# Weight splits held behind a norm's vector steps, the mean square summed on ScalarE, attention weights scaled on ScalarE

## The chip, the core and the metric

The kernel runs on one core of a Trainium2 chip. The core has a matrix engine (TensorE; PE in the profile, PEld being its weight loads), a vector engine (VectorE, DVE), an engine for activations (ScalarE, ACT), a general one (GpSimd, POOL) and one that only issues transfers (SyncE, SP). Each engine works through its own queue in order, and they wait for one another by semaphores. The metric is the device time of one execution in microseconds.

## What is computed

Two transformer blocks, 256 tokens of width 1024, everything in fp32. The first block has two layers, the second one. Cut to what matters here:

```python
for l in range(2):                                   # first block
    h = rms_norm(x, g_pre_mix[l])
    q, k, v, cb, cc, cx, ga, gb = split(h @ w_in[l])
    y_attn = band_attention(rope(q), rope(k), v, sink[l]) @ w_attn_proj[l]
    y_conv = (cb * short_conv(cc * cx, conv_w[l])) @ w_conv_proj[l]
    mix = (sigmoid(ga) * y_attn + sigmoid(gb) * y_conv) @ w_out[l]
    x = x + rms_norm(mix, g_post_mix[l])
    h = rms_norm(x, g_pre_ffn[l])
    x = x + rms_norm((silu(h @ w_gate[l]) * (h @ w_up[l])) @ w_down[l], g_post_ffn[l])
# second block: the same frame, norms modulated by a condition vector
# (h = rmsnorm(x) * (1 + scale) + shift), stick-breaking attention and a pooling mixer

def rms_norm(x, g):
    return x * rsqrt(mean(x * x, axis=-1) + 1e-6) * g

# in band_attention, per block of 128 queries and head
p = exp(sc - m)
denom = sum(p, axis=-1) + exp(sink - m)
o = (p / denom) @ v
```

## The kernel before

**Weights.** All weights are packed into a list of chunks of 128 x 2048 fp32 (1 MB), in the order of their use (`ORDER`). `emit_raw` (L242) loads a chunk into one of four buffers on SyncE's queue. `emit_split` (L252) splits it into a high part H (rounded to the matrix engine's fp32r by ScalarE, L265) and a low part L (the rest, a subtraction on VectorE, L266), in two halves of 128 x 1024; there are nine buffers for halves of H and nine for L. A product is then three matmuls: high by high, low by high, high by low. `get(key)` (L271) hands out the next chunk, and before that emits the loads up to five chunks ahead (`LOOK_RAW`) and the splits up to three ahead (`LOOK`, counting the chunk itself). Chunks called `cond` belong to the second block's condition and are not split: VectorE sums them (L490), GpSimd reduces the sum (L493).

**Order.** The program is traced in one order, and a scheduler then places each engine's instructions: among those that its own timing model has ready it takes the one with the earliest place in the program, as far as buffers allow. `hp()` moves the norm steps 30 places forward. Work that comes from generators (transposes, attention units) is traced into TensorE's stream at due times of a clock that counts matmul time (`spawn`, `tick`); TensorE's order is that of the trace.

**A boundary.** There are five places at which an output product is followed by a norm, the residual, another norm and the next weights: mixer to FFN in layers 0 and 1 (`mix_out`, L461), FFN to the next mixer after layers 0 and 1 (`ffn`, L496), and the second block's output projection to its FFN (L951 to L965). `row_out` (L450) ends the output product for the first row tile of 128 tokens, then for the second one. After each half of the columns `Post.half` squares the result on ScalarE (`sumsq`, L331, tiles `jk_a..`) and multiplies it by the gain (L391, `ag`). After a row tile, `after` calls `post.fin` (inverse root on GpSimd: `rstd`, L333, three small operations `ms`, `m` and `rs`; then x is updated, L398) and `Norm.vec` (squares of x, L331; gain, L356, `xg`; inverse root; scale, L360 or L362), and spawns the transposes of that tile (`Norm.tr`, L371, `pt_n..`) for 6 us later by the program's clock (`TR_DELAY`). The transposed rows are split again (`Pair.put`, L201 and L202). The FFN starts with chunks `gA` and `uA` (two each), each used for both row tiles.

**Attention.** `attention` (L560) spawns eight units per layer, one per group of four heads and row tile, every 10 us of the clock. A unit splits and transposes q (`qs`, `qT`), computes scores S, masks them and takes the maximum on VectorE, takes four exponentials of 128 x 256 on ScalarE with their sums (L628), one more of the sink (L630, `es`), the reciprocal on VectorE (L631, L633, `rd`), multiplies the four tiles P by it on GpSimd (L635), transposes P on TensorE (L643, `PTp`) 8 us of the clock later, and multiplies by v. The units run between the matmuls of the convolution branch (`pcc`, `pcx`, `pcb`).

## Time and profile before

| | us |
|---|---|
| three timed runs, median (lowest, highest) | 1191.44 (1191.36, 1191.72) |
| the profiled execution, device time | 1194.28 |
| its span, first to last instruction | 1192.4 |
| TensorE busy | 1159.4 (97%) |
| VectorE busy | 773.1 (65%) |
| ScalarE busy | 618.3 (52%) |
| GpSimd busy | 129.1 (11%) |

The page gives busy times for the whole span. A busy TensorE says that a matmul was in work, not that it ran at full clock, so the granted clock is read beside it. A row of a timeline has the start, the time from the start of the first to the end of the last of its merged instructions, the engine, the line, the operation with its output and inputs, and in brackets how long the engine was idle before it and who ended that. Successive instructions overlap a little at their ends.

### The profile page before, as it was taken

To read this page: it belongs to the slowest core of one execution; us is meant where nothing else is said; L and a number is where in the kernel's file an instruction comes from. 1 tells how busy PE (TensorE), PEld (TensorE's weight loads), DVE (VectorE), ACT (ScalarE), POOL (GpSimd) and SP (SyncE) were. 2 spreads that over 40 slices of the span, in tenths; PEclk is the share of its full clock that TensorE was granted. 3 is DMA by queue.
4 is the path that set the end of the run, shared out by engine and by line. 5 is a ranking of instruction groups with operands and counts; after the bars stand their busy time and mean duration, and the time that the engine had idled before them with its cause. 6 is when DMAs were issued, how large, how long until landed. Compare 5 with 4: busy or idle time off the path is not lost.

```text
span 1192.4 us, 17771 instructions
## 1 busy us (share of the span) xinstructions
PE 1159.4 (97%) x7144; PEld 1029.3 (86%) x7144; DVE 773.1 (65%) x958; ACT 618.3 (52%) x927; POOL 129.1 (11%) x146
## 2 busy tenths in 40 slices
PE   6999999999999999999999999999999999999997
PEld 4899888878999987998888878999988777999996
DVE  6768655769576747677747768776858448655542
ACT  5756556555444346656556555344455546544441
POOL 1012300011202001022220022020211002000000
PEclk9999999999999999999999999999999999999999
DMA  8743344757676665634438547675866345655620
GB/s 307 284 135 114 111 147 177 271 181 259 231 258 239 226 233 181 243 106 142 142 142 316 185 169 257 230 290 180 315 230 222 120 159 177 247 177 177 206 77 36
DMA packets 36250, 235.50 MB, mean 197 GB/s; under 512 B 4668, under 2 KB 5180, under 8 KB 9416
## 3 DMA queue, kind: packets, MB, share of 16 engines
q1 hardware_dynamic: 33696, 225.41, 53.2%
q10 hardware_dynamic: 2472, 8.96, 2.3%
q8 instruction: 56, 0.92, 0.3%
q14 instruction: 26, 0.21, 0.1%
HBM read 233.28 MB, written 1.07 MB: 197 GB/s over the span
## 4 chain that ended last, share of the span: by engine, by line
PE 51%; POOL 2%; ACT 1%; DVE 1%; issue 1%; POOLq 0%; ACTq 0%; DVEq 0%
PE pu L236 10%; PE dn L236 9%; PE pg L236 8%; PE wo L236 2%; PE pcp L236 2%; PE pap L236 2%; PE pga L236 2%; PE pgb L236 2%; PE pcx L236 2%; PE pcb L236 1%; PE puA L236 1%; PE pgA L236 1%; PE z L236 1%; PE po L236 1%; PE pv L236 1%
## 5 line engine op out<-in xcount | busy, mean ns | idle before, releaser
L266 DVE TENSOR_TENSOR L<-raw,H 128x1024 fp32r<-128x1024 f32 x374 | 470.1, 1264 | 218.6 <-ACT H L265 207.7
L265 ACT CAST H<-raw 128x1024 fp32r<-128x1024 f32 x374 | 391.0, 1050 | 321.3 <-PE pu L236 71.5
L236 PE MATMUL dn<-H,fHL 128*128 128x512 f32 x432 | 116.4, 391 | 0.0
L236 PEld LDWEIGHTS dn<-H,fHL 128*128 128x128 f32 x432 | 79.8, 188 | 15.6
L635 POOL TENSOR_SCALAR P<-P,rd 128x256 f32<-128x256 f32 x64 | 48.2, 769 | 228.9 <-DVE rd L633 83.7
L236 PE MATMUL dn<-L,fHL 128*128 128x512 f32 x216 | 66.8, 390 | 0.0
L493 POOL PARTITION_ALL_REDUCE mrow<-cacc x6 | 40.1, 6675 | 219.5 <-DVE cacc L490 180.8
L490 DVE SCALAR_TENSOR_TENSOR cacc<-raw,silu_c,cacc 128x1024 f32<-128x1024 f32 x48 | 61.4, 1280 | 0.3
L236 PEld LDWEIGHTS dn<-L,fHL 128*128 128x128 f32 x216 | 40.5, 188 | 8.5
L536 DVE TENSOR_TENSOR f<-pu,s 128x512 f32<-128x512 f32 x27 | 18.6, 690 | 30.1 <-PE pu L236 30.1
L628 ACT ACTIVATE P<-S,nm 128x256 f32<-128x256 f32 x64 | 29.6, 478 | 11.8 <-DVE nm L622 11.8
L539 ACT CAST fHL<-f 128x512 fp32r<-128x512 f32 x27 | 16.8, 622 | 36.1 <-DVE f L536 36.1
L236 PE MATMUL pg<-xf2H,H 128*128 128x256 f32 x144 | 35.4, 283 | 0.0
L236 PE MATMUL pg<-xf0H,H 128*128 128x256 f32 x144 | 35.4, 283 | 0.0
L236 PE MATMUL pg<-xf1H,H 128*128 128x256 f32 x144 | 35.3, 283 | 0.0
L236 PE MATMUL pu<-xf0H,H 128*128 128x256 f32 x144 | 35.3, 283 | 0.0
L236 PE MATMUL pu<-xf0L,H 128*128 128x256 f32 x144 | 35.3, 283 | 0.0
L236 PE MATMUL pu<-xf1H,H 128*128 128x256 f32 x144 | 35.3, 283 | 0.0
L236 PE MATMUL pu<-xf1L,H 128*128 128x256 f32 x144 | 35.3, 283 | 0.0
L236 PE MATMUL pu<-xf2H,H 128*128 128x256 f32 x144 | 35.3, 283 | 0.0
L236 PE MATMUL pu<-xf2L,H 128*128 128x256 f32 x144 | 35.3, 283 | 0.0
L236 PE MATMUL pg<-xf0L,H 128*128 128x256 f32 x144 | 35.3, 283 | 0.0
(402 smaller groups left out, 2928.2 us busy)
## 6 DMA issues: line engine op xcount, KB each, us to landing
raw<-in_wpack_dram SPq DMA_DIRECT2D x209, 1024.0 KB, 5.0
raw<-in_wpack_dram SPq DMA_DIRECT2D x4, 512.0 KB, 8.9
gpm<-in_gains_dram ACTq DMA_DIRECT2D x3, 512.0 KB, 6.0
gpf<-in_gains_dram ACTq DMA_DIRECT2D x3, 512.0 KB, 7.0
gqf<-in_gains_dram ACTq DMA_DIRECT2D x2, 512.0 KB
out_dram<-x SPq DMA_DIRECT2D x4, 256.0 KB, 2.1
pmat<-in_pmat_dram SPq DMA_DIRECT2D x2, 384.0 KB, 5.6
x<-in_x_dram SPq DMA_DIRECT2D x2, 256.0 KB, 2.6
```

The costliest lines, as they stand in the source:

```text
L236: nc.tensor.matmul(o, a, b, start=start, stop=stop, **kw)
L265: nc.scalar.copy(H, rv)
L266: nc.vector.tensor_sub(L, rv, H.bitcast(F32))
L490: nc.vector.scalar_tensor_tensor(a3, w[:, k], silu_c[:, 2 * j + k:2 * j + k + 1], a3, ALU.mult, ALU.add)
L493: nc.gpsimd.partition_all_reduce(mrow, a, P, bass_isa.ReduceOp.add)
L536: nc.vector.tensor_mul(f, pu, s)
L539: nc.scalar.copy(fHL[:, 0], fv)
L628: nc.scalar.activation(Pt[:, hh, :], S[hh // 2][:, hh % 2, :], AF.Exp, bias=nm[:, hh:hh + 1], accum_out=den[:, hh:hh + 1])
L635: nc.gpsimd.tensor_scalar(Pt[:, hh, :], Pt[:, hh, :], rd[:, hh:hh + 1], 0.0, ALU.mult, ALU.add)
```

## The change

`get` takes a second argument that limits how far ahead it splits: at the five boundaries the output product's chunks are split, and nothing behind them. A new function `split_ahead` splits the next two chunks, and is called in `after` for the first row tile, once its `Norm.vec` has been traced; `issue_after` orders the casts on ScalarE behind the last instruction of that norm's sum of squares, and the subtractions on VectorE behind the last scaling. `sumsq` scales x by 1/32 inside the square, and a second ScalarE instruction on 128 x 1 (Identity with a bias) adds epsilon or the first half's sum; on GpSimd only the power is left. The multiplication of the attention weights goes from GpSimd to ScalarE.

```diff
@@ -268,16 +268,24 @@
             HL[i] = hv
         state["spl"] += 1
 
-    def get(key):
+    def get(key, look=LOOK):
         i = state["use"]
         assert ORDER[i] == key, (ORDER[i], key)
         n = len(ORDER)
         while state["raw"] < min(i + LOOK_RAW, n):
             emit_raw()
-        while state["spl"] < min(i + LOOK, n):
+        while state["spl"] < min(i + min(look, LOOK), n):
             emit_split()
         state["use"] += 1
         return HL.pop(i)
+
+    def split_ahead(*behind):
+
+        with ExitStack() as st:
+            for ins in behind:
+                st.enter_context(tc.issue_after(ins.ins))
+            while state["spl"] < min(state["use"] + LOOK - 1, len(ORDER)):
+                emit_split()
 
 
     HC = [slice(0, 512), slice(512, 1024)]
@@ -300,6 +308,8 @@
     nc.sync.dma_start(xt[1], x_in[P:2 * P, :])
     nhalf = cst.tile([P, 1], F32, tag="nhalf", name="nhalf")
     nc.vector.memset(nhalf, -0.5)
+    eps = cst.tile([P, 1], F32, tag="eps", name="eps")
+    nc.vector.memset(eps, EPS)
     ident_r = cst.tile([P, P], F32R, tag="identr", name="ident_r")
     nc.vector.tensor_copy(ident_r, ident)
     modd = dr.tile([6, D], F32, tag="modd", name="modd")
@@ -327,16 +337,15 @@
 
 
     def sumsq(src, c, ssq, name):
+
         junk = s2(f"jk_{name}{c}")
-        nc.scalar.activation(junk, src, AF.Square, accum_out=ssq[:, c:c + 1])
+        nc.scalar.activation(junk, src, AF.Square, scale=D ** -0.5, accum_out=ssq[:, c:c + 1])
+        return nc.scalar.activation(ssq[:, c:c + 1], ssq[:, c:c + 1], AF.Identity,
+                                    bias=eps if c == 0 else ssq[:, 0:1])
 
     def rstd(ssq, name):
-        ms = small("ms_" + name, 1)
-        nc.gpsimd.tensor_scalar(ms, ssq[:, 0:1], 1.0 / D, EPS, ALU.mult, ALU.add)
-        m2 = small("m2_" + name, 1)
-        nc.gpsimd.tensor_scalar(m2, ssq[:, 1:2], 1.0 / D, ms[:, 0:1], ALU.mult, ALU.add)
         rs = small("rs_" + name, 1)
-        nc.gpsimd.tensor_tensor(rs, m2, nhalf, ALU.pow)
+        nc.gpsimd.tensor_tensor(rs, ssq[:, 1:2], nhalf, ALU.pow)
         return rs
 
     class Norm:
@@ -352,14 +361,14 @@
                 ssq = small("sx_" + name, 2)
                 xg = s4("xg_" + name)
                 for c in range(2):
-                    sumsq(xt[t][:, HC[c]], c, ssq, "x" + name)
+                    self.sq = sumsq(xt[t][:, HC[c]], c, ssq, "x" + name)
                     nc.vector.tensor_mul(xg[:, HC[c]], xt[t][:, HC[c]], self.G[:, HC[c]])
                 rs = rstd(ssq, "x" + name)
                 for c in range(2):
                     if self.S is None:
-                        nc.vector.tensor_scalar(xg[:, HC[c]], xg[:, HC[c]], rs[:, 0:1], None, ALU.mult)
+                        self.sc = nc.vector.tensor_scalar(xg[:, HC[c]], xg[:, HC[c]], rs[:, 0:1], None, ALU.mult)
                     else:
-                        nc.vector.scalar_tensor_tensor(xg[:, HC[c]], xg[:, HC[c]], rs[:, 0:1], self.S[:, HC[c]],
+                        self.sc = nc.vector.scalar_tensor_tensor(xg[:, HC[c]], xg[:, HC[c]], rs[:, 0:1], self.S[:, HC[c]],
                                                        ALU.mult, ALU.add)
             self.h = xg
 
@@ -461,13 +470,14 @@
     def mix_out(l, kts, mp, make_post, after, lead):
         accs = [[ps1(f"wo{l}_{t}{c}") for c in range(2)] for t in range(2)]
         for i, j in enumerate(kts[:lead]):
-            w = get(("wo", l, j))
+            w = get(("wo", l, j), len(kts) - i)
             tick()
             for t in range(2):
                 for c in range(2):
                     mmD2(accs[t], w, mp.ks(0, 2 * j, 2), mp.ks(1, 2 * j, 2), t, c, i == 0, False)
         drain()
-        ch = [(get(("wo", l, j)), mp.ks(0, 2 * j, 2), mp.ks(1, 2 * j, 2)) for j in kts[lead:]]
+        ch = [(get(("wo", l, j), len(kts) - i), mp.ks(0, 2 * j, 2), mp.ks(1, 2 * j, 2))
+              for i, j in enumerate(kts) if i >= lead]
         row_out(ch, accs, lead > 0, make_post, after)
 
     cacc = [None]
@@ -550,7 +560,7 @@
                         for c in range(2):
                             mmD2(accs[t], w, fs[j][0], fs[j][1], t, c, j == 0, False)
                 else:
-                    tail.append((get(key), fs[j][0], fs[j][1]))
+                    tail.append((get(key, NDOWN - j), fs[j][0], fs[j][1]))
         if l == DEPTH - 1:
             with tc.issue_after(last.ins):
                 nc.scalar.preload_act_table_set("natural_log_exp_and_others")
@@ -632,7 +642,7 @@
             rd = small(f"rd{l}{g}{t}", 4)
             nc.vector.reciprocal(rd, den)
             for hh in range(4):
-                nc.gpsimd.tensor_scalar(Pt[:, hh, :], Pt[:, hh, :], rd[:, hh:hh + 1], 0.0, ALU.mult, ALU.add)
+                nc.scalar.activation(Pt[:, hh, :], Pt[:, hh, :], AF.Copy, scale=rd[:, hh:hh + 1])
             yield SM_DELAY
             if t == 0:
                 PT[g] = [s4(f"PT{l}{g}{pr}", (P, 2, 2, T)) for pr in range(2)]
@@ -879,6 +889,8 @@
         def after(t, post):
             post.fin()
             norms[t].vec()
+            if t == 0:
+                split_ahead(norms[t].sq, norms[t].sc)
             spawn(norms[t].gen, TR_DELAY)
 
         mix_out(l, [0, 1, 2, 3], mp, lambda t, acc: Post(t, acc, gpm, f"pm{l}{t}"), after, LEAD)
@@ -909,6 +921,8 @@
         def after2(t, post):
             post.fin()
             nn[t].vec()
+            if t == 0:
+                split_ahead(nn[t].sq, nn[t].sc)
             spawn(nn[t].gen, TR_DELAY)
 
         ffn(l, xp, norms, mkpost, after2)
@@ -946,6 +960,8 @@
     def after3(t, post):
         post.fin()
         norms[t].vec()
+        if t == 0:
+            split_ahead(norms[t].sq, norms[t].sc)
         spawn(norms[t].gen, TR_DELAY)
 
     accs = [[ps1(f"wo2_{t}{c}") for c in range(2)] for t in range(2)]
@@ -954,7 +970,7 @@
         for c in range(2):
             mmD2(accs[t], *pw[i], t, c, i == 0, False)
     drain()
-    aw = [(get(("wo", 2, j)), mp.ks(0, 2 * j, 2), mp.ks(1, 2 * j, 2)) for j in (0, 1)]
+    aw = [(get(("wo", 2, j), 2 - j), mp.ks(0, 2 * j, 2), mp.ks(1, 2 * j, 2)) for j in (0, 1)]
     for t in range(2):
         post = Post(t, accs[t], Pm, f"pm2{t}")
         left = pw[max(0, WO2_LEAD - 2):] if t == 1 else []
```

## Rows read from the trace of the kernel before

**Rows 1.** The page, part 1: busy us, share of the span, instructions.

```profile
PE 1159.4 (97%) x7144; PEld 1029.3 (86%) x7144; DVE 773.1 (65%) x958; ACT 618.3 (52%) x927; POOL 129.1 (11%) x146
```

**Rows 2.** TensorE's waits: who for whom, us in total, times, longest.

```profile
PE pt_n L371 <- DVE xg_n L360: 9.5, 1, 9.5
PE PTp L643 <- POOL P L635: 6.4, 6, 1.6
PE pt_nf L371 <- DVE xg_nf L360: 2.6, 2, 1.3
```

**Rows 3.** TensorE's timeline around two attention units of layer 0.

```profile
75.93 0.60 PE L643 MATMUL PTp<-ident,P 128*128 128x128 f32 x4
78.09 1.00 PE L643 MATMUL PTp<-ident,P 128*128 128x128 f32 x4 [1.56 <-POOL P L635]
78.85 0.36 PE L236 MATMUL S<-kTh,qT 128*128 128x256 f32 x1
...
124.53 0.33 PE L643 MATMUL PTp<-ident,P 128*128 128x128 f32 x1 [0.28 <-POOL P L635]
...
127.45 0.38 PE L236 MATMUL pcc<-x0H,H 128*128 128x256 f32 x1
```

**Rows 4.** The chain that ended last: start, us, what, count.

```profile
533.44 0.87 PE PTp L643 x8
...
616.73 21.76 PE pgb L236 x96
```

**Rows 5.** Windows: length; busy us (count) by engine; clock, DMA share, GB/s.

```profile
79.90:83.30 3.40, 3.40 (x19) 3.40 (x18) 2.17 (x6) 0.61 (x2) 0.00 (x0) 0.50 0.26 108
84.30:87.70 3.40, 3.40 (x31) 3.40 (x31) 1.68 (x3) 3.19 (x12) 0.00 (x0) 1.00 0.28 41
```

**Rows 6.** Line 635 (ns min/median/max), then GpSimd and VectorE in one unit.

```profile
L635 POOL TENSOR_SCALAR P<-P,rd x64: 476/484/2570, 74.0 to 599.3; 128x256 f32<-128x256 f32 x64
...
74.03 4.46 POOL L635 TENSOR_SCALAR P<-P,rd 128x256 f32<-128x256 f32 x4 [55.46 <-ACT y0H L201]
...
75.41 2.36 DVE L266 TENSOR_TENSOR L<-raw,H 128x1024 fp32r<-128x1024 f32 x2 [0.74 <-ACT H L265]
```

**Rows 7.** ScalarE: one group (busy, mean ns), timeline with a reciprocal, one window.

```profile
L855 ACT ACTIVATE m2H<-ppl,pscale 128x256 fp32r<-128x256 f32 x4 | 1.9, 476 | 3.2 <-PE ppl L236 3.2
...
70.11 1.28 ACT L628 ACT_TABLE_LOAD   x1
74.31 2.02 ACT L265 CAST H<-raw 128x1024 fp32r<-128x1024 f32 x2
86.26 0.21 ACT L630 ACTIVATE es<-es 128x4 f32<-128x4 f32 x1
88.12 0.18 DVE L633 RECIPROCAL rd<-den 128x4 f32<-128x4 f32 x1
...
57.00:109.00 52.00, 50.31 (x411) 48.77 (x410) 38.04 (x82) 33.55 (x74) 9.82 (x14) 0.97 0.38 132
```

**Rows 8.** The first boundary, timeline and windows; a split at the second.

```profile
256.77 0.60 ACT L331 ACTIVATE jk_apm<-wo 128x512 f32<-128x512 f32 x1 [3.39 <-PE wo L236]
261.64 1.22 DVE L266 TENSOR_TENSOR L<-raw,H 128x1024 fp32r<-128x1024 f32 x1
262.77 0.82 POOL L337 TENSOR_SCALAR m_xnf<-sx_nf,ms_xnf 128x1 f32<-128x1 f32 x1 [2.26 <-ACT jk_xnf L331]
264.27 0.88 DVE L360 TENSOR_SCALAR xg_nf<-xg_nf,rs_xnf 128x512 f32<-128x512 f32 x2 [0.81 <-POOL rs_xnf L339]
264.81 0.66 PE L371 MATMUL pt_nf<-ident,xg_nf 128*128 128x128 f32 x4 [1.28 <-DVE xg_nf L360]
...
250.50:256.70 6.20, 6.20 (x29) 5.15 (x28) 0.69 (x1) 0.69 (x2) 0.19 (x1) 1.00 0.41 160
265.20:273.40 8.20, 8.20 (x41) 6.69 (x40) 7.15 (x10) 4.43 (x10) 2.91 (x5) 1.00 0.39 130
...
433.56 1.22 DVE L266 TENSOR_TENSOR L<-raw,H 128x1024 fp32r<-128x1024 f32 x1
```

## The prediction

> **What bounds the kernel now.** I read the page first: TensorE is busy for 1159.4 of 1192.4 us [rows 1], so whatever is to be won lies in some 33 us of its idle time and in stretches where it runs slowly. Then its waits [rows 2]: 9.5 us at the start for the first input, which the change hardly touches; 6.4 us for attention weights (L643, `PTp`) that GpSimd scales at L635; and the transposes L371 behind a norm, on two lines and two names (2.6 us is the first of them). Those are five waits of the size of the one at 264.81, 1.28 us [rows 8], 6.7 us in all. Then the timeline of TensorE around the two attention waits of layer 0 [rows 3]; layer 1 repeats both in the same form, so there are four. In the first, eight transposes begin at 75.93 and the next work at 78.85: 2.92 us, where eight normally take 0.87 [rows 4], so 2.05 us are lost. In the second it is 127.45 - 124.53 = 2.92, again 2.05 lost, and 0.28 of idle time before it: 2.33.
>
> The windows show a second loss behind each [rows 5]. In 79.90 to 83.30 TensorE counts as fully busy, but its granted clock is 0.50 (1.2 of 2.4 GHz) and it does 19 matmuls; with the clock back at 1.00 the same 3.40 us hold 31. That is 12 x 3.40/31 = 1.3 us. What the engine did before it fell: it stood idle for 1.56 us within the transposes [rows 3]. Behind the norm wait at 264.81 the clock stays at 1.00 [rows 8].
>
> So attention loses 2 x (2.05 + 2.33) + 4 x 1.3 = 8.8 + 5.2 = 14.0 us, the norms 6.7.
>
> **Part 1: attention weights on ScalarE.** 64 GpSimd operations go. Alone one takes 0.48 us, but the slowest took 2.57 [rows 6]: the four that began at 74.03 took 4.46 us together, while VectorE ran two subtractions of 1.2 us each beside them. ScalarE gets 64 copies with a scale per partition. No row has this very form; the nearest is L855, an ACTIVATE of the same 128x256 with such a scale, 476 ns [rows 7]. From below, a quarter of a 128x1024 cast is 2.02/8 = 0.25 us [rows 7]; I take the upper end, which is the same shape: 4 x 0.48 = 1.9 us a unit, where 1.0 is the lower end. A unit whose reciprocal is ready at 74.0 then has its weights by 75.9 if the scale comes next on ScalarE, and by 78.0 if the two casts at 74.31 (2.02 us) stand before it [rows 7]. TensorE asks for the second half of them at about 75.93 + 0.87/2 = 76.4. I take the first, because the scheduler that sets the order takes what is ready and earliest in the program, and these come straight after the reciprocal. The gain is then all 14.0 us; if they come behind the casts it is about nothing.
>
> It is paid on ScalarE: 64 x 0.48 = 31 us. In 57 to 109 us ScalarE is busy 33.55 of 52, VectorE 38.04 [rows 7]; four units there add 7.7, so ScalarE comes to 41.2 of 52. It stays below TensorE, so the throughput hides it; order doesn't always. ScalarE works in order, and the scale waits for VectorE's reciprocal: in the second unit ScalarE ends its exponentials at 86.26 + 0.21 = 86.47 and the reciprocal comes at 88.12 [rows 7], so 1.65 us of idle time and 1.9 of scales stand before whatever is queued behind them: weight casts (H, needed many us later) and `qT`, which the next unit's score matmuls need soon. Bounds: 0 if the scheduler puts `qT` first, 16 units x 0.5 = 8 us if each exposes a small part. I take 1.5. Sum of this part: -14.0 + 1.5 = -12.5 (from -14 to +1).
>
> By the Trainium skill (ScalarE: Activation LUTs, Rules for kernel authors) a multiplication should go to VectorE and not to ScalarE, which speaks against this step; what it would do here is the first of the rivals below. In the trace VectorE is the busier of the two engines in this stretch, so that rule weighs little here.
>
> **Part 2: mean square on ScalarE.** Per norm two small GpSimd operations go, and two ACTIVATEs of 128x1 (Identity) come. The closest row is L630, 0.21 us [rows 7]. Of the removed two only the second is on the chain; the one at 262.77 took 0.82 us beside a VectorE subtraction [rows 8]. The power stays on GpSimd. Alone it is an even trade (0.21 and a hand-over within ScalarE against one GpSimd step of the same order), against contention it wins up to 0.6. No row has Identity; COPY and CAST run among the exponentials with no table load between, and I take the same for it: bounds -0.6 to +0.2 on each chain. If it needed a load, each would cost 1.28 [rows 7]. The Trainium skill (ScalarE: Activation LUTs, Table sets: the hidden batching unit) says that identity lies in every set as filler; no row here shows it.
>
> **Part 3: splits behind the norm.** There are five boundaries: mixer output to FFN in layers 0 and 1, FFN to the next mixer twice, and the second block's output projection to its FFN. At each, the first row tile's post-norm and pre-norm run while TensorE works on the second row tile, and its transposes are fixed in TensorE's order 6 us (of the program's own clock) later. At the first boundary the chain runs from 256.77 to 265.15 [rows 8]: 8.4 us. Two weight subtractions (L266, 1.22 each; one is shown at 261.64) and the slow GpSimd step stand inside; without them it takes 8.4 - 2 x 1.14 - 0.4 = 5.7 to 6.3. TensorE was idle from 264.81 - 1.28 = 263.53, 6.8 us after the start: so the wait of the first row tile goes at all five boundaries, -6.7 at most.
>
> What comes in its place: splits that were done in idle VectorE time now come after the norm. In 250.5 to 256.7 VectorE is busy for 0.69 of 6.20 us, the splits then allowed being done; in 265.2 to 273.4 it is busy for 7.15 of 8.20 [rows 8]. The change takes three halves out of the former (as many as found a free buffer before 250.5) and puts them into the latter: 3 x 1.22 = 3.7 us against 1.05 free. What is queued behind a held split: on VectorE the multiplication for the second row tile's post-norm and the low parts of the transposed rows; on ScalarE the casts and that tile's squares, though the norm steps have priority. Who waits: `gA` and `uA` on TensorE, which eat a half in 6 matmuls, 6 x 21.76/96 = 1.36 us [rows 4], and the second row tile's transposes. SP is moved too: a weight buffer is free only after its subtraction, so the request for the chunk four later goes out some 15 us later; it is wanted two row tiles of `gA` and `uA` (four passes) later, so this hides, with less in hand. GpSimd only loses work.
>
> At the two mixer-to-FFN boundaries I expect the late halves to cost 3.7 - 1.05 - 0.6 (the GpSimd step) = 2.0 us against the 1.4 gained: +0.6 each. At the other three only one half was split early (433.56 at the second boundary [rows 8]), the second row tile's matmuls last a third longer, and I expect 0.2 to 0.4 of new waiting against 1.4: -1.1 each. Sum: 1.2 - 3.3 = -2.1. Bounds: -6.7 if the later chunks, which carry no wait, fill the idle stretch instead; on the other side nine halves (two boundaries by three, three by one) of 1.22 exposed, 11.0 - 6.7 = +4.3.
>
> **Sum.** -12.5 - 2.1 = -14.6, part 2 being within the chains. The profiled execution took 1194.28 us for a span of 1192.4, 1.9 us lying around it; it is 2.84 above the median of the three timed runs, 1191.44. Against its own time the forecast is 1194.3 - 14.6 = 1179.7; against the median, 1191.4 - 14.6 = 1176.8.
>
> **The rivals.**
>
> *ScalarE gets late in attention.* The four waits go, but 16 units each lose 0.5 us at `qT`, and a clock drop follows once per layer (2 x 1.3): -14.0 + 8 + 2.6 - 2.1 = -5.5, so 1185.9. For it: the 1.65 us of idle waiting in the second unit, at the head of an in-order queue. Against it: ScalarE has 18 of 52 us free.
>
> *Splits become late.* Each mixer-to-FFN boundary loses 3 us and then a clock drop of 1.3, the others keep what they lost: -12.5 + 2 x (4.3 - 1.4) = -6.7, so 1184.7. For it: VectorE's 7.15 of 8.20. Against it: other chunks can be moved up into idle time.
>
> *The attention part doesn't do what it says.* The scales stand behind the two casts, and the weights come as late as before: 0 - 2.1, so 1189.3.
>
> *Slower.* Place: the five boundaries. Mechanism: all four held halves (4 x 1.22 = 4.9 us) are exposed on TensorE at each, with the clock falling behind it (1.3), against 1.4 won: +4.8 each, +24; with attention's -12.5 that is 1202.9. It decides once a boundary loses more than (12.5 + 2.4)/5 = 3.0 us net. Against it: before the second row tile's matmuls end, VectorE has room for at least two of the four.
>
> **How the numbers follow.** Chances: forecast 0.56, late ScalarE 0.14, late splits 0.13, attention unchanged 0.08, slower 0.09. A difference under 0.2% (2.4 us) can't be told from none, so 1189.3 lies at the edge of that: of its 0.08 I count 0.06 as the same. Faster is 0.56 + 0.14 + 0.13 + 0.02 = 0.85, the same 0.06, slower 0.09. The likeliest case's own range is 1170 (attention whole, norms whole: -14 - 6.7 = -20.7) to 1183. Taking in the two late cases, 1170.5 to 1187 leaves out the last two and the lowest edge, under 2 in 10.
>
> **What would show it.** Right: no TensorE wait for `P` at L643, four fewer stretches at clock 0.50, GpSimd with 128x1 powers and its all-reduces only; the transposes L371 of a first row tile without a wait; no H or L between a first row tile's squares. Wrong: waits of `S` on `qT` (late ScalarE), of `gA`, `uA`, `pq` on `L` or of a second row tile's L371 longer than 1 us with clock 0.50 behind them (late splits), or `PTp` waiting for ScalarE (unchanged).

## The result, and the profile after

| | before | after |
|---|---|---|
| median (lowest, highest), us | 1191.58 (1191.36, 1193.47) | 1185.13 (1183.56, 1185.96) |
| after to before, 95% interval | | 0.994 (0.9928 to 0.9952) |
| the profiled execution, device time | 1194.28 | 1185.07 |
| its span, us | 1192.4 | 1183.3 |
| ScalarE busy, us | 618.3 | 650.5 |
| GpSimd busy, us | 129.1 | 63.0 |

The change makes the kernel 6.5 us faster (5.7 to 8.6 by the interval), where 14.6 were forecast: inside the range, and at the place of the rival "splits become late" (1184.7). Part 1 of the page of after, to be read beside [rows 1]:

```profile
PE 1155.1 (98%) x7144; PEld 1026.4 (87%) x7144; DVE 771.8 (65%) x959; ACT 650.5 (55%) x1039; POOL 63.0 (5%) x34
```

TensorE's waits of after (who for whom, us in total, times, longest), beside [rows 2]:

```profile
PE pt_n L380 <- DVE xg_n L369: 9.2, 1, 9.2
PE ptf L515 <- DVE sA L530: 2.6, 1, 2.6
PE puA L236 <- ACT H L265: 2.1, 2, 1.0
PE pt_nm L380 <- DVE xg_nm L369: 1.2, 1, 1.2
PE pt_nf L380 <- DVE xg_nf L371: 1.1, 1, 1.1
PE pt_nm L380 <- DVE xg_nm L371: 1.1, 1, 1.1
```

The wait of `PTp` is gone from the list. Of the norm waits those of the first row tile are gone too; the three at L380 that are left (1.2, 1.1, 1.1) belong to a second row tile. New are `puA` waiting for `H` and `ptf` waiting for `sA`.

TensorE runs the same 7144 matmuls in both kernels, in the same order but for some 80 places, nearly all at the boundaries, where transposes stand a few matmuls earlier or later. So the i-th matmul of after can be set against the i-th of before. What this lag gains or loses in each stretch, from the two profiled executions:

| stretch | after minus before, us | forecast |
|---|---|---|
| start | -0.4 | 0 |
| attention, layer 0 | -7.6 | -6.25 |
| boundary 1, mixer to FFN | +2.5 | +0.6 |
| boundary 2, FFN to mixer | 0 | -1.1 |
| attention, layer 1 | -7.6 | -6.25 |
| boundary 3, mixer to FFN | +4.8 | +0.6 |
| boundaries 4 and 5 | -0.7 | -2.2 |
| all, to the last matmul | -9.0 | -14.6 |

The sum is 9.0 and not 6.5 because before's profiled execution stood 2.7 above the median; what the runs show of that is told under the last heading. So attention gave more than forecast, and the boundaries, forecast at -2.1, cost 6.6.

### The profile page after: what moved, and what is told of

Same layout as the page of the kernel before. It is cut to its first block, busy times and chain, and to the rows that moved or that the text cites. A ratio compares the mean times of both kernels' runs of the same rounds, so it can differ in the third digit from the quotient of the medians.

```text
span 1183.3 us, 17669 instructions
## 1 busy us (share of the span) xinstructions
PE 1155.1 (98%) x7144; PEld 1026.4 (87%) x7144; DVE 771.8 (65%) x959; ACT 650.5 (55%) x1039; POOL 63.0 (5%) x34
## 4 chain that ended last, share of the span: by engine, by line
PE 55%; ACT 3%; DVE 1%; DMA 1%; POOL 1%; issue 0%; DVEq 0%; POOLq 0%; ACTq 0%
PE pu L236 10%; PE dn L236 9%; PE pg L236 9%; PE wo L236 2%; PE pcb L236 2%; PE pcx L236 2%; PE pcc L236 2%; PE pcp L236 2%; PE pap L236 2%; PE pga L236 2%; PE pgb L236 2%; ACT H L265 1%; PE pgA L236 1%; PE pq L236 1%; PE puA L236 1%; PE z L236 1%
## 5 line engine op out<-in xcount | busy, mean ns | idle before, releaser
L236 PE MATMUL pg<-xf1L,H 128*128 128x256 f32 x144 | 36.2, 288 | 0.0
L236 PE MATMUL pg<-xf2L,H 128*128 128x256 f32 x144 | 35.3, 283 | 0.0
```

Of the source, the lines that this page charges most:

```text
L236: nc.tensor.matmul(o, a, b, start=start, stop=stop, **kw)
```

## Attention, as the trace of after shows it

The timeline of one unit of layer 0 in after, VectorE, ScalarE and TensorE (start, us, engine, line, operation, idle time before it and who ended it), beside [rows 3] and [rows 6]:

```profile
73.43 0.18 DVE L643 RECIPROCAL rd<-den 128x4 f32<-128x4 f32 x1
...
73.70 1.71 ACT L645 ACTIVATE P<-P,rd 128x256 f32<-128x256 f32 x4
75.32 0.56 ACT L618 CAST qT<-pq 128x512 fp32r<-128x512 f32 x1
...
75.69 1.03 PE L653 MATMUL PTp<-ident,P 128*128 128x128 f32 x8
76.48 0.36 PE L236 MATMUL S<-kTh,qT 128*128 128x256 f32 x1
```

The scales come next on ScalarE behind the reciprocal, as the prediction chose, and the four take 1.71 us (4.46 on GpSimd beside VectorE's subtractions, [rows 6]). They end at 75.41, TensorE transposes all eight blocks in one go, and `qT`, put behind the scales, ends at 75.88, 0.6 us before the score matmuls use it. The window of [rows 7] and the first one of [rows 5], in after:

```profile
57.00:109.00 52.00, 52.00 (x441) 50.87 (x440) 39.68 (x84) 40.88 (x92) 0.00 (x0) 1.00 0.39 136
...
79.90:83.30 3.40, 3.40 (x31) 3.40 (x30) 3.40 (x5) 3.40 (x12) 0.00 (x0) 1.00 0.35 92
```

ScalarE is busy for 40.88 of 52 us (forecast 41.2), TensorE is never idle, and 79.90 to 83.30 holds 31 matmuls at a granted clock of 1.00 (2.4 GHz), where [rows 5] showed 19 at 0.50.

## Boundary 1, as the trace of after shows it

ScalarE, VectorE and TensorE around the transposes, beside [rows 8]:

```profile
255.68 1.99 ACT L265 CAST H<-raw 128x1024 fp32r<-128x1024 f32 x2
257.57 0.57 ACT L201 CAST xf0H<-pt_nf 128x512 fp32r<-128x512 f32 x1
...
258.63 1.04 ACT L265 CAST H<-raw 128x1024 fp32r<-128x1024 f32 x1
...
256.32 3.48 DVE L266 TENSOR_TENSOR L<-raw,H 128x1024 fp32r<-128x1024 f32 x3
259.73 0.68 DVE L202 TENSOR_TENSOR xf0L<-pt_nf,xf0H 128x512 fp32r<-128x512 f32 x1
...
255.37 0.60 PE L380 MATMUL pt_nf<-ident,xg_nf 128*128 128x128 f32 x4
...
258.20 0.49 PE L236 MATMUL pgA<-H,xf0H 128*128 128x512 f32 x1 [0.41 <-ACT xf0H L201]
259.72 0.49 PE L236 MATMUL puA<-H,xf0H 128*128 128x512 f32 x1 [1.03 <-ACT H L265]
260.46 0.59 PE L236 MATMUL pgA<-H,xf0L 128*128 128x512 f32 x1 [0.24 <-DVE xf0L L202]
```

The transposes at 255.37 wait for nothing: the first half of the plan worked. They end at 255.97, and the cast of their result, `xf0H`, can start on ScalarE then, but starts at 257.57, because two held casts of weights began at 255.68 and ScalarE takes its queue in order. VectorE has begun three held subtractions at 256.32 and reaches the rows' own, `xf0L`, at 259.73. The second matmul behind the transposes is one of `puA`, and the cast of its weight, queued behind the held ones, starts at 258.63. TensorE stands idle for 0.41, 1.03 and 0.24 us, 1.68 in all against 1.28 before [rows 8], and then its clock falls. Three windows, the second behind the transposes of boundary 3, the third some 30 us later:

```profile
260.70:264.10 3.40, 3.40 (x9) 2.62 (x9) 3.40 (x7) 3.34 (x8) 0.32 (x1) 0.50 0.99 402
696.50:699.90 3.40, 3.40 (x16) 2.77 (x17) 3.40 (x6) 3.26 (x8) 0.35 (x1) 1.00 1.00 419
725.20:728.20 3.00, 3.00 (x15) 3.00 (x16) 2.74 (x3) 0.59 (x1) 0.00 (x0) 0.50 0.93 380
```

In the first the clock is 0.50 (1.2 GHz), for 9 matmuls of 512 columns; at 2.4 GHz six of them take 1.36 us [rows 4], so the 9 need 2.04 and 1.36 us are lost. 1.68 + 1.36 - 1.28 = 1.8 of the table's 2.5. Behind each of the three idle times the lag also grows by some 0.2 us more than the idle time; the rest is not accounted for.

## Boundary 3: the same, and a reduction of GpSimd

VectorE, GpSimd and TensorE of after:

```profile
712.64 6.70 DVE L266 TENSOR_TENSOR L<-raw,H 128x1024 fp32r<-128x1024 f32 x2
...
724.39 0.68 DVE L530 TENSOR_TENSOR sA<-puA,sA 128x512 f32<-128x512 f32 x1
...
712.92 6.93 POOL L503 PARTITION_ALL_REDUCE mrow<-cacc  x1 [10.23 <-PE pgA L236]
...
725.13 1.12 PE L515 MATMUL ptf<-ident,sA 128*128 128x128 f32 x4 [2.65 <-DVE sA L530]
```

Behind the transposes TensorE waits here as at boundary 1 (0.53, 1.03 and 0.31 us, 1.87 in all), but its clock stays at 1.00 (696.50 to 699.90 above). Some 20 us later two subtractions of VectorE take 6.70 us beside GpSimd's sum over partitions of the condition (alone one takes 1.22 [rows 8]), four more follow, and `sA`, the FFN's first product, comes 2.65 us late. The clock falls behind that (0.50 in 725.20 to 728.20 above). The kernel before has the same meeting, with a smaller wait (VectorE's timeline, then TensorE's waits):

```profile
722.10 5.88 DVE L266 TENSOR_TENSOR L<-raw,H 128x1024 fp32r<-128x1024 f32 x2 [0.47 <-ACT H L265]
...
PE ptf L505 <- DVE sA L520: 0.6, 1, 0.6
```

1.87 + 2.65 + 1.3 (the clock) - 1.3 - 0.6 (the two waits of before) = 3.9; the table has 4.8, and the rest is of the kind left over at boundary 1.

## Experiments

Ratios are to the kernel before, run on the same chip.

| kernel | what it has | median, us | ratio (95%) |
|---|---|---|---|
| e1_attn_only | attention scale alone | 1178.60 | 0.9889 (0.9874 to 0.9904) |
| e2_hold_only | held splits alone | 1198.16 | 1.0055 (1.004 to 1.007) |
| e3_meansq_only | mean square alone | 1192.94 | 1.000 (0.999 to 1.001) |
| e4_no_hold | change without held splits | 1179.52 | 0.9898 (0.9883 to 0.9913) |
| f1_hold_late | hold not at mixer to FFN | 1180.39 | 0.9897 (0.9877 to 0.9916) |
| f2_rows_first | change, rows first | 1177.72 | 0.9875 (0.9859 to 0.9891) |
| f3_no_reduce3 | change, one reduction less | 1181.34 | 0.9906 (0.9887 to 0.9925) |
| f4_attn_delay | e1, transposes later | 1182.45 | 0.9917 (0.9898 to 0.9936) |
| g1_attn_vector | attention scale on VectorE | 1181.29 | 0.991 (0.9893 to 0.9926) |
| g2_rows_no_hold | e4, rows first | 1179.93 | 0.990 (0.9885 to 0.9915) |
| g3_hold_rows | e2, rows first | 1195.06 | 1.0025 (1.0009 to 1.004) |
| h1_all_first | change, all norm steps first | 1178.83 | 0.9885 (0.9868 to 0.9901) |

**e1_attn_only: the attention part alone, on before.**

```diff
-nc.gpsimd.tensor_scalar(Pt[:, hh, :], Pt[:, hh, :], rd[:, hh:hh + 1], 0.0, ALU.mult, ALU.add)
+nc.scalar.activation(Pt[:, hh, :], Pt[:, hh, :], AF.Copy, scale=rd[:, hh:hh + 1])
```

> The kernel before with one part of the change: attention weights scaled on ScalarE. Theory (the attention part does all that it was priced at, and the held splits give part of it back): the four waits for P and the stretches at clock 0.50 behind them go, 14 us in the trace of before; its timed runs lie 2.8 us below its traced one, so 1177 to 1180 timed, ratio 0.988 to 0.990. Rival (ScalarE gets late in attention, the boundaries cost nothing): no better than the whole change, 1184 to 1187.

Measured 0.9889: 13 us, more than all three parts together. Its trace has no wait of `PTp`, and no clock drop until the last matmuls. The five first-row-tile waits stand as before, 1.2 to 1.5 us each.

**e2_hold_only: the held splits alone.** `get`'s limit and `split_ahead` of the change, with the old mean square on GpSimd and the old attention scale. Of the edit to the kernel after, the attention scale:

```diff
-nc.scalar.activation(Pt[:, hh, :], Pt[:, hh, :], AF.Copy, scale=rd[:, hh:hh + 1])
+nc.gpsimd.tensor_scalar(Pt[:, hh, :], Pt[:, hh, :], rd[:, hh:hh + 1], 0.0, ALU.mult, ALU.add)
```

> The kernel before with the held splits alone (mean square and attention weights stay on GpSimd). Theory: the five boundaries cost 5 to 7 us more than before, so 1196 to 1199, with TensorE waiting for the transposed rows' casts at the two mixer-to-FFN boundaries. Rival (boundaries cost nothing): 1190 to 1192. If the mean square on ScalarE is what makes the boundaries late, this one is 1188 to 1191.

Measured 1.0055: the hold alone costs 5 to 8 us. TensorE's waits show the same two places as in after:

```profile
PE ptf L514 <- DVE sA L529: 2.7, 1, 2.7
PE pgA L236 <- DVE xf0L L202: 1.6, 1, 1.6
```

**e3_meansq_only: the mean square alone.** The edit to the kernel before, in part; the two GpSimd operations of `rstd` go as in the change.

```diff
-nc.scalar.activation(junk, src, AF.Square, accum_out=ssq[:, c:c + 1])
+nc.scalar.activation(junk, src, AF.Square, scale=D ** -0.5, accum_out=ssq[:, c:c + 1])
+return nc.scalar.activation(ssq[:, c:c + 1], ssq[:, c:c + 1], AF.Identity, bias=eps if c == 0 else ssq[:, 0:1])
```

> The kernel before with the mean square on ScalarE alone. Theory: within 1 us of before (1190.5 to 1192.5), the chain to the norm's scale being shorter only where a GpSimd step stood beside a VectorE subtraction. Rival (it is the small ScalarE instructions that make the boundaries late): 1195 or more.

Measured 1.000 (0.999 to 1.001): nothing. The three parts alone add up to -11.1 + 5.5 + 0 = -5.6 thousandths, and together they measured -6.0, so within these intervals they don't act on each other in sum.

**e4_no_hold: the change without its third part.** The edit to the kernel after, in part:

```diff
-def get(key, look=LOOK):
+def get(key):
...
-            if t == 0:
-                split_ahead(norms[t].sq, norms[t].sc)
```

> The changed kernel without the held splits: mean square and attention weights on ScalarE, splits as far ahead as before. Theory: 1176 to 1180, so faster than the changed kernel by 5 to 8. Rival (ScalarE late in attention): 1184 to 1187, like the changed kernel.

Measured 0.9898 against 0.994 with the hold: in the company of the other parts the hold costs some 5 us. The first row tiles wait 0.8 to 1.0 us here, some 0.4 less than in e1 (one GpSimd step less on the chain), but 0.4 to 0.7 us then turn up at the second row tile or at the first weights, so that nothing is won in the sum.

**f1_hold_late: the hold kept at boundaries 2, 4 and 5 alone.** The edit to the kernel after, in part:

```diff
-w = get(("wo", l, j), len(kts) - i)
+w = get(("wo", l, j))
...
-            if t == 0:
-                split_ahead(norms[t].sq, norms[t].sc)
```

> The changed kernel with the splits held at three boundaries only (FFN to the next mixer twice, second block's projection to its FFN); the two mixer-to-FFN boundaries as before. Theory (the loss sits at the two mixer-to-FFN boundaries, 2.0 and 4.8 us in the trace, the other three are even): the 6 to 7 us come back, 1178 to 1181, ratio 0.988 to 0.991. Rival (every boundary loses about the same): two fifths come back, 1182 to 1184.

Measured 0.9897 (e4: 0.9898), as without any hold. So, within some 2 us, the whole cost of the hold is at the two mixer-to-FFN boundaries, and at the other three it is worth nothing.

**f2_rows_first: the change, with the transposed rows' cast and subtraction ahead of the held splits in priority.**

```diff
-                with hp():
+                with nullcontext() if state["use"] == 0 else tc.high_priority(offset=120):
                     self.xp.put(4 * j, 4, pt, ts_)
```

> The changed kernel with the transposed rows' own cast and subtraction put ahead of the held weight splits (120 places forward instead of 30). Theory (queue order: at the mixer-to-FFN boundary the rows wait behind weight casts and subtractions that are wanted later): TensorE's waits for xf0H, xf1H, H and xf L at the two boundaries, 1.7 and 1.9 us, go to under 0.7 each, with the clock drop behind the first where there is one; 1181 to 1183.5. Rival (VectorE has no room, whatever the order): the wait moves from the rows to the weights' L, or to the second row tile's transposes, and the time stays at 1184 to 1186.

Measured 0.9875, 1177.72 us: some 7 us under the change. Only the priority of these casts and subtractions was edited. But with it the scheduler placed three queues anew: those of ScalarE and VectorE and, at the two mixer-to-FFN boundaries, TensorE's, whose order is therefore not only that of the trace, as the section on the kernel before has it. The matmul of `puA` that stands second behind the transposes in before and after stands 23 places later here. Boundary 1 in its timeline, beside that of after above:

```profile
256.66 0.58 ACT L201 CAST xf0H<-pt_nf 128x512 fp32r<-128x512 f32 x1
...
258.63 0.68 DVE L202 TENSOR_TENSOR xf0L<-pt_nf,xf0H 128x512 fp32r<-128x512 f32 x1
...
257.60 0.48 PE L236 MATMUL pgA<-H,xf0H 128*128 128x512 f32 x1
259.37 0.50 PE L236 MATMUL pgA<-H,xf0L 128*128 128x512 f32 x1 [1.29 <-DVE xf0L L202]
...
264.69 0.39 PE L236 MATMUL puA<-H,xf0H 128*128 128x512 f32 x1
```

`xf0H` comes 0.9 us sooner against its transposes, `xf0L` 1.1; three idle times of 1.68 us in all have become one of 1.29, and no clock drop follows. At boundary 3 `sA` now stands on VectorE in front of the subtraction that meets the reduction (it starts at 716.60, in after at 724.39), and the wait of `ptf` for it is gone. In the lag, boundaries 1 and 3 come to +0.2 and -0.4 us where after has +2.5 and +4.8, and all five to -0.9 against the trace of before, where -2.1 were forecast. How much of this is ScalarE's order, VectorE's or TensorE's, no run separates.

**f3_no_reduce3: the change without one GpSimd reduction.** The reduction of condition row 3 is left out, and that row's sum is set to 0.

```diff
-            nc.gpsimd.partition_all_reduce(mrow, a, P, bass_isa.ReduceOp.add)
+            if r == 3:
+                nc.vector.memset(mrow, 0.0)
+            else:
+                nc.gpsimd.partition_all_reduce(mrow, a, P, bass_isa.ReduceOp.add)
```

> The changed kernel without GpSimd's all-reduce of the condition's row 3 (its result is set to zero), the one that runs beside the first FFN weights of layer 1. Theory (that all-reduce holds up VectorE's subtractions, and with the splits late there is no margin left for it): the wait of 2.65 us for sA and the clock drop behind it go, 1180.5 to 1182.5. Rival (VectorE is late by the splits alone): the wait stays above 1.5 us, 1184 to 1186.

Measured 0.9906, 3.8 us under the change. In its trace the 2.65 us of `sA` and the clock drop behind them are gone (boundary 3 comes to +0.5 us in the lag), and VectorE's two subtractions at that place take the normal time. Boundary 1 has the same order on TensorE and ScalarE as in after and the same three idle times, and yet no clock drop (1.00 in the last row); it comes to +1.2 us where after has +2.5:

```profile
711.70 2.35 DVE L266 TENSOR_TENSOR L<-raw,H 128x1024 fp32r<-128x1024 f32 x2
...
258.58 0.49 PE L236 MATMUL pgA<-H,xf0H 128*128 128x512 f32 x1 [0.41 <-ACT xf0H L201]
260.11 0.50 PE L236 MATMUL puA<-H,xf0H 128*128 128x512 f32 x1 [1.03 <-ACT H L265]
260.84 0.50 PE L236 MATMUL pgA<-H,xf0L 128*128 128x512 f32 x1 [0.23 <-DVE xf0L L202]
...
261.10:264.50 3.40, 3.40 (x16) 2.79 (x16) 3.40 (x7) 3.34 (x8) 0.32 (x1) 1.00 0.95 381
```

**f4_attn_delay: e1 with the transposes 7.5 us behind the norm in place of 6.**

```diff
-TR_DELAY = 6.0
+TR_DELAY = 7.5
```

> The kernel before with attention weights on ScalarE, no held splits, and the norm's transposes placed 1.5 us later in TensorE's order (TR_DELAY 7.5 instead of 6). Theory (the waits of 1.3 us at the five boundaries come from a place in TensorE's order that is too early by about that much): the five go or shrink below 0.5, 1173 to 1176 against 1178.6 for the same kernel with 6.0. Rival (the first products behind the transposes are then late by the same amount): 1178 to 1180.

A miss: the waits were thought to go away if the transposes only stood later, and it came out at 1182.45, slower than e1. The waits at the transposes go in part, but the rows then reach the first weights late:

```profile
PE pgA L236 <- DVE xf0L L202: 1.4, 1, 1.4
```

With it comes one of 1.2 us for `xf0H`. The same 1.3 us or so turn up at the next place that needs the norm. What waits is the chain, and not where TensorE first asks for it.

**g1_attn_vector: e1 with the scale on VectorE.**

```diff
-nc.scalar.activation(Pt[:, hh, :], Pt[:, hh, :], AF.Copy, scale=rd[:, hh:hh + 1])
+nc.vector.tensor_scalar(Pt[:, hh, :], Pt[:, hh, :], rd[:, hh:hh + 1], None, ALU.mult)
```

> The kernel before with the scale of the attention weights on VectorE in place of ScalarE. What the gain of the attention part rests on is either that GpSimd, whose operation stretches from 0.48 to 2.57 us beside VectorE's subtractions, is left; or that ScalarE, with its idle time, takes the work. First theory (leaving GpSimd is enough): no wait of PTp, 1177 to 1181 us, as with ScalarE alone (1178.6). Rival (VectorE is the fuller engine, and a scale stands behind one or two subtractions of weights of 1.2 us each): half of the weights come 1 to 2 us late in some units, PTp waits remain with a clock drop behind some, 1183 to 1188. The Trainium skill (ScalarE: Activation LUTs, Rules for kernel authors) would have the multiplication on VectorE.

Measured 0.991 against 0.9889 with ScalarE; the intervals overlap. No `PTp` waits, but one of 0.82 us for `qs` of VectorE at 575.99 in layer 1, that e1 doesn't have. The line of the scale, its shortest, median and longest duration in ns, in g1:

```profile
L635 DVE TENSOR_SCALAR P<-P,rd x64: 341/348/354, 74.7 to 585.3; 128x256 f32<-128x256 f32 x64
```

and in e1:

```profile
L635 ACT ACTIVATE P<-P,rd x64: 492/497/551, 74.2 to 584.9; 128x256 f32<-128x256 f32 x64
```

So most of the gain (10.7 of 13.2 us by the ratios) comes from leaving GpSimd, whose longest was 2570 ns [rows 6], and what hangs on which engine takes it lies within the intervals. The rule of the Trainium skill (ScalarE: Activation LUTs, Rules for kernel authors), a multiplication belongs on VectorE, agrees with the duration of one instruction (348 against 497 ns) and not with the kernel's time, which isn't less for it.

**g2_rows_no_hold: no hold, rows first.** The edit of f2 on e4.

```diff
-                with hp():
+                with nullcontext() if state["use"] == 0 else tc.high_priority(offset=120):
```

> The changed kernel without held splits, and with the transposed rows' cast and subtraction 120 places ahead in priority in place of 30. It tells what the hold is worth once the rows come first. Theory (the order of the queue was the loss; the hold itself wins the first row tile's waits, some 1 us at each boundary, and the second's take most of it back): the first row tile's waits of 0.8 to 1.0 us remain, 1177.5 to 1180, within 2 us of the version with rows first and hold (1177.72). Rival (the hold pays its full 1.3 us a boundary once the rows come first): 1183 to 1185, 5 to 7 us above that version. Other rival (priority alone is what won): 1173 to 1176, under that version.

Measured 1179.93 (0.990), as e4 without the edit (1179.52). Priority alone wins nothing. With it, the hold is worth 0.990 - 0.9875 = 2.5 thousandths, 3 us; the intervals overlap, so its size is not well known.

**g3_hold_rows: the hold alone, rows first.** The edit of f2 on e2.

```diff
-                with hp():
+                with nullcontext() if state["use"] == 0 else tc.high_priority(offset=120):
```

> The kernel before with held splits alone, and the transposed rows' cast and subtraction 120 places ahead in priority. With 30 places the held splits alone cost 5 to 7 us (1198.2 against 1191 to 1193). Theory (their cost is that they stand ahead of the rows in ScalarE's and VectorE's order): the cost goes, no wait of gA or uA for H, none of sA in layer 1, and the time is 1188 to 1192. Rival (the cost is the work put off itself, which finds no room on VectorE, in whatever order): waits move to L or to the rows, and it stays at 1196 to 1199.

Half a miss: 1195.06 and not 1188 to 1192. The edit takes 3 thousandths off e2 (1.0055 to 1.0025) and the wait for `sA` is gone, but the hold alone still costs some 3 us in the median. In the profiled execution, which took 1191.08 and has one clock drop among its attention stalls, the five boundaries lose about 1 us against before; the executions themselves ran from 1191.1 to 1198.3. What the others lost more, no trace shows. So with rows first the hold wins some 3 us in f2's company and costs some 3 us alone; why, these runs leave open.

**h1_all_first: the change, with every norm step 120 places ahead.**

```diff
-PRIO = 30
+PRIO = 120
```

> The changed kernel with every norm step (squares, scales and the rows' cast and subtraction) 120 places ahead in priority, in place of 30. It asks whether the waits of 1.3 to 1.6 us that are left at the second row tile's transposes, with the rows alone put first, come of the place in the queue too. In the order of ScalarE and VectorE this moves the second row tile's squares and its two scalings ahead of held casts and subtractions at the two mixer-to-FFN boundaries; at the other three the casts that stand ahead of the second row tile's squares stay there, because a cast is ready while that row tile's matmuls still run, and no priority holds it back. Theory (such waits come of held casts that run before the squares become ready, which priority doesn't change): the waits of the other three boundaries stay between 1.1 and 1.7 us, and the time is within 1.5 us of the version with the rows alone put first, 1176.2 to 1179.2. Rival (place in the queue): they fall under 0.5 us each, 1172 to 1175.

Measured 1178.83, within 1.1 us of f2, and the waits at the second row tile's transposes of boundaries 2, 4 and 5 stay where they were in f2 (1.3, 1.6 and 1.6 us in either):

```profile
PE pt_nm L380 <- DVE xg_nm L371: 1.6, 1, 1.6
```

That fits the theory: priority picks among what is ready, and a held cast that is ready before the squares are isn't kept back by it.

## Boundaries 2, 4 and 5: where the other waits went

At these the forecast was -1.1 each and the measured gain is nothing (f1 against e4). The first row tile's wait did go; the second row tile's transposes wait instead. Boundary 2 in after, from the last `dn` matmul, which ends at 450.2, to the transposes:

```profile
451.04 0.60 ACT L342 ACTIVATE jk_apf<-dn 128x512 f32<-128x512 f32 x1
...
451.62 1.06 ACT L265 CAST H<-raw 128x1024 fp32r<-128x1024 f32 x1
452.56 0.31 ACT L343 ACTIVATE sa_pf<-sa_pf 128x1 f32<-128x1 f32 x1
...
456.29 1.40 POOL L348 TENSOR_TENSOR rs_xnm<-sx_nm,nhalf 128x1 f32<-128x1 f32 x1 [2.80 <-ACT sx_nm L343]
...
456.06 1.22 DVE L266 TENSOR_TENSOR L<-raw,H 128x1024 fp32r<-128x1024 f32 x1
457.72 0.88 DVE L369 TENSOR_SCALAR xg_nm<-xg_nm,rs_xnm 128x512 f32<-128x512 f32 x2 [0.44 <-POOL rs_xnm L348]
...
458.26 0.66 PE L380 MATMUL pt_nm<-ident,xg_nm 128*128 128x128 f32 x4 [1.25 <-DVE xg_nm L369]
```

and the same chain in before, where these transposes have no wait:

```profile
457.75 0.59 ACT L331 ACTIVATE jk_apf<-dn 128x512 f32<-128x512 f32 x1
...
462.37 0.55 POOL L339 TENSOR_TENSOR rs_xnm<-m_xnm,nhalf 128x1 f32<-128x1 f32 x1
...
462.95 0.89 DVE L360 TENSOR_SCALAR xg_nm<-xg_nm,rs_xnm 128x512 f32<-128x512 f32 x2 [0.80 <-POOL rs_xnm L339]
```

From the start of the square to the start of the scaling it took 5.2 us in before and takes 6.7 now. A held cast stands between the square and the new small sum on ScalarE (451.62, about 0.9 us), and GpSimd's power takes 1.40 beside a held subtraction where it took 0.55 (0.85 us). So the mean square's new step on ScalarE, an even trade in the time of e3, is hit by the held casts: parts 2 and 3 meet here. Each of them alone already makes such waits: the second row tile's transposes at boundaries 2, 4 and 5 wait 0, 0 and 0.29 us in before, 0.74, 0.46 and 0.29 in e3, 0.70, 0.67 and 0.76 in e2, and 1.25, 1.08 and 1.08 in after. At boundary 5 the power starts within three held subtractions and ends 0.4 us after the last of them; alone it took 0.55:

```profile
994.12 3.48 DVE L266 TENSOR_TENSOR L<-raw,H 128x1024 fp32r<-128x1024 f32 x3
...
994.43 3.58 POOL L348 TENSOR_TENSOR rs_xnf<-sx_nf,nhalf 128x1 f32<-128x1 f32 x1 [2.89 <-ACT sx_nf L343]
```

How much the cast in between and how much the slow power weigh there was not tried.

## Why the prediction was right and wrong, step by step

- *Attention loses 14.0 us, and scaling on ScalarE gives -12.5.* Right, if somewhat low. The lag table has 15.2 for the two layers, e1 alone 13.2 by its ratio (interval 11.4 to 15.0), and the scale came straight behind the reciprocal. The 1.5 us allowed for a late ScalarE were not needed: `qT` is in time, 40.88 of 52 us are as forecast. The nearest row, 476 ns, stood for 497.
- *The mean square, nothing.* Right by itself (e3, 1.000). Identity on 128x1 took 0.28 to 0.31 us for the 0.21 of the nearest row, and it brought no table load: ten in either trace. What was missed is that its place on ScalarE lies open to whatever is queued there, the held casts above all, at the second row tile.
- *The first row tile's wait goes.* Right: no wait at 255.37, and the chain of boundary 1 takes 254.66 - 248.77 = 5.9 us from its first square to the end of its scaling, where 5.7 to 6.3 were forecast.
- *Each mixer-to-FFN boundary +0.6.* This step failed; measured are +2.5 and +4.8. It asked how much time VectorE had free for three late halves (1.05 us) and took the rest as the loss. The runs show a loss of order in its place: ScalarE, which is idle enough, has held casts in front of the row's own cast and of the weight that TensorE wants second, and VectorE held subtractions in front of the row's own. The prediction names casts and subtractions as queued behind a held split, and then lets the norm's priority see to it; 30 places don't reach past splits traced earlier than the rows, 120 do. f2 changes that priority alone, has +0.2 and -0.4 at these boundaries, and recovers some 7 us. Of the same 7 us, and not on top of them, f3 recovers 3.8 by another way: the reduction at boundary 3, which meets VectorE's subtractions in before already (0.6 us), is a term that the prediction left out. Two clock drops are in it as well.
- *Each of the other three -1.1.* This failed too: nothing won within some 2 us (f1 against e4), as the second row tile took over the wait. The 0.2 to 0.4 us allowed for new waiting were 1.25, 1.08 and 1.08.
- *The rival "splits become late".* The time it gave, 1184.7, was met partly by luck. It has +2.9 for each mixer-to-FFN boundary, a clock drop among it, where the two measured 2.5 and 4.8, and nothing won at the others, which is about right. But it takes attention at -12.5 where the traces have -15.2, and it sets terms read from the profiled execution of before against a median that stood 2.7 lower; these two cancel. Its reason, the fullness of VectorE, was not what decided: in f2 the same splits are held as long and cost little.
- *SP's later requests hide.* No wait of TensorE names a transfer in after.
- *The median of before.* The forecast used -14.0 for attention with four clock drops, from one execution. Not every execution has four (below), so part of that term isn't there in the median: e1 has 13.2 by its ratio against 15.2 in the traces.

Settled is that the loss at the mixer-to-FFN boundaries goes when the rows are put in front, since that priority alone was edited (f2), the loss lies at these two boundaries (f1), and the same edit without the hold wins nothing (g2). Not settled is how the loss divides among the orders of ScalarE, VectorE and TensorE, and why the hold alone still costs some 3 us with rows first (g3). That the clock drop at boundary 1 comes of the three idle times just before it is not shown: boundary 3 of after and boundary 1 of f3 have such idle times without a drop. The best time, 1177.72 us of f2, is under e1's 1178.60, but their intervals overlap.

## What to carry to other kernels

When work is moved behind a wait on an in-order engine, list what will be queued behind it and what comes out of the wait in the same microsecond; the room that the engine has on average doesn't answer that. Held work that is traced earlier than the row it competes with needs a lower place than that row on every engine that both use; and as a change of priority can reorder TensorE's queue too, compare that order as well. And before work is moved to where GpSimd and VectorE meet, look for GpSimd's longest rows there, not for their median.

## What the runs showed of the hardware

- **GpSimd beside VectorE's subtractions.** GpSimd's power of 128x1 took 0.55 us alone, 1.40 beside one subtraction and 3.58 beside three in a row, ending some 0.4 us after the last. The other way round, two subtractions took 6.70 us beside a reduction of 6.93, and 2.35 without it (f3). The Trainium skill (SBUF — State Buffer, Terms) says that the two arbitrate for a port pair which one holds for a whole instruction while the other blocks. The rows agree on the blocking; that it lasts for the whole instruction they show only roughly, as the second of the two subtractions ended 0.5 us before the reduction's recorded end (719.34 against 719.85). And they show more: a waiting GpSimd operation can stand behind several of VectorE's in a row.
- **The clock drops are not the same in each execution.** Before's profiled execution has four stretches at granted clock 0.50 inside the kernel, e3's with the same attention stalls two, g3's one. Beside e1, executions of before ran from 1190.9 us at a mean clock of 0.996 to 1194.1 us at 0.993. In after, a drop follows idle times of 0.41, 1.03 and 0.24 us at boundary 1, and none follows 0.53, 1.03 and 0.31 at boundary 3; in f3 none follows 0.41, 1.03 and 0.23 at boundary 1, and in e1 none follows idle times of 1.24 to 1.45 at the boundaries. So the length of the last idle time doesn't tell by itself, and a single profile may hold more of such drops than the median.
